# A two-layer trunk on one core: u tiles held two behind, low parts of weights made by POOL, output loads on SP

## The chip, the cores and the metric

The kernel runs on one core of one Trainium2 chip. Its engines are TensorE (PE, matrix products, with its weight loads PEld), VectorE (DVE), ScalarE (ACT), GpSimd (POOL) and SyncE (SP), which here only issues DMAs. Each engine works through its own list of instructions in order, and waits at an instruction until what it needs is there. The metric is the device time of one execution in microseconds (us), and of several executions the median.

## The reference

A trunk of two layers over a sequence of 1024 positions of width 1024. Layer 0 is a gated linear attention (GLA), layer 1 an S5 state space model; both have a cross attention into a memory beside the sequence mixer, a gate and an output projection.

```python
h = rms_norm(x, norm_w[i])                 # i = 0: GLA, i = 1: S5
u, z, xq = split_cols(h @ w_in, [2048, 3072, 1024])   # S5 layer
# S5: 128 groups of 16 columns with 64 complex states, in chunks of 128 steps
bu = einsum('bcgh,gph->bcgp', u, bb)       # into the states
x_t = ab * x_{t-1} + bu_t                  # recursion
y = Re(c x) + d * u
y = gelu(y); y = y * sigmoid(y @ w_glu + b_glu)
x = x + (concat([y, memory_attention(xq)]) * silu(z)) @ w_out[i]
```

After layer 1 a last RMSNorm gives the output. All is float32.

## The kernel before

A float32 product is made of three faster ones: both factors are split into a high part (rounded to a format that PE takes at full rate) and a low part (the rest), and high x high, high x low and low x high are summed (`mm3`, L78 to 86 in the class `Trunk`). For weights `unit()` does it: it loads a tile of 128x1024 (`wr`, three buffers, SP's queue, L78), ACT makes the high part `wh` (L69), and the low part `wl` is the subtraction `wr - wh` on DVE (L70). PE then does 48 products with such a unit, 24 for each half of the 1024 positions.

The order in which each engine does its instructions is made when the kernel is built: a scheduler simulates the program and puts instructions that are ready into an engine's list. Tiles come from pools with a number of buffers, and pools that are opened later reuse the memory of pools that are done; a tile then waits until the last use of what lay there. An explicit order (`behind`, `add_manual_dep`) keeps one instruction of an engine behind another. `self.made` is POOL's last store of the operators that it makes for the S5 stage (`od`, made by L770 to L775: two products into `op` and `opt`, their sum, a store).

The S5 stage, `s5()`, is where the diff lies:

- 16 units `w_su` make u, in two parts of eight tiles (`PARTS`; tiles 0 to 3 and 8 to 11, then the rest). Each tile is stored (`ud`, L919) and loaded again ordered by step (`uu`, L921).
- `states()` loads two operator tiles (`rt` into `rtp`, L902), lets PE multiply them with `uu` (L905, 16 products a tile, two blocks of eight), and ACT copies the result into the state tile `st`. The list `held` says how many tiles of u it lags behind the projections.
- The recursion over the 127 steps after the first runs on DVE, three operations a step (L932, L934, L936), for each part in two independent chains of 16 groups. The first chain of part 0 needs the tiles 0, 1, 8 and 9, the second the tiles 2, 3, 10 and 11.
- The outputs, per tile of u in two groups: loads of `uq` (u again), `tp` (into the tag `rtp`) and `ow` (from `od`), ACT and DVE make `xg` from the states, PE adds two products (L959 and L960), ACT makes the gelu (L961), SP stores (`y1`).
- 16 units `w_sz` make the gates: ACT a tanh (`zt`), DVE the product `zs` (L270), SP stores it.

Then `glu()` multiplies y with the last weight of the S5 layer. The scheduler mixes all of these: gates are projected while the recursion runs.

Of the kernel before, what the change touches and what calls it, by code (L numbers as in the profile page):

```python
# [8 lines left out]
F32 = mybir.dt.float32  # L9
# [7 lines left out]
P = 128  # L17
# [28 lines left out]
class Trunk:  # L46
# [19 lines left out]
    def split(self, h, l, src, scale=None, eng=None):  # L66
        nc = self.nc
        if scale is None:
            nc.scalar.copy(h, src)  # L69
            (eng or nc.vector).tensor_tensor(l, src, h.bitcast(F32), ALU.subtract)  # L70
        else:
            nc.scalar.activation(h, src, AF.Copy, scale=scale)
            nc.vector.scalar_tensor_tensor(l, src, scale, h.bitcast(F32), ALU.mult, ALU.subtract)

    def unit(self, src):

        raw = self.stream.tile([P, 1024], F32, tag="wr", name="wr")
        self.nc.sync.dma_start(raw, src)  # L78
        h = self.stream.tile([P, 1024], F32R, tag="wh", name="wh", bufs=2)
        l = self.stream.tile([P, 1024], F32R, tag="wl", name="wl", bufs=2)  # L80
        self.split(h, l, raw)
        return h, l

    def mm3(self, out, ah, al, bh, bl, first, last):
# [803 lines left out]
    def s5(self, xs, zs_d, y1_d):  # L888
# [3 lines left out]
        with ExitStack() as ctx:  # L892
            st = [self.pool(ctx, f"st{i}").tile([P, 2, 32, P + 1], F32, name=f"st{i}") for i in range(2)]
            sp = self.tags(ctx, "s5")
            for part in range(2):
# [13 lines left out]
                            nc.scalar.copy(st[part][hp, ri, g0:g0 + 4, 1:], pv[64 * ri:64 * ri + 64])  # L909

                held = []
                for j in self.PARTS[part]:
                    ub = sp.tile([P, 8, P], F32, tag="uy", name="uy", bufs=3)
                    u = self.unit(t["w_su"][j])
                    for hf in range(2):
                        ps = self.ps()
                        self.gemm(ps, u, xs[hf])
                        nc.scalar.copy(ub[:, :, 64 * hf:64 * hf + 64], ps.rearrange("p (s c) -> p s c", s=8))
                    nc.sync.dma_start(ud[j].rearrange("s p c -> p s c"), ub)  # L919
                    uu = sp.tile([P, 8, P], F32, tag="uu", name="uu", bufs=2)  # L920
                    nc.sync.dma_start(uu, by_step[j])  # L921
                    held.append((j, uu))
                    if len(held) > 1:
                        states(*held.pop(0))
                states(*held.pop())
                a2 = self.a2[:, :, :, 32 * part:32 * part + 32]
                chains = [slice(16 * i, 16 * i + 16) for i in range(2)]
                for c in range(2, P + 1):
# [8 lines left out]
            for part in range(2):  # L937
                for j in self.PARTS[part]:
                    half, jl = divmod(j, 8)
                    hp = slice(64 * half, 64 * half + 64)  # L940
                    yo = sp.tile([P, 8, P], F32, tag="uy", name="uy", bufs=3)
                    for q in range(2):
                        n, hb = 2 * jl + q, slice(4 * half, 4 * half + 4)
                        uq = sp.tile([P, 4, P], F32, tag="uq", name="uq", bufs=2)
                        loads = [nc.gpsimd.dma_start(uq, by_step[j][:, 4 * q:4 * q + 4, :])]  # L945
                        tp = sp.tile([P, 4, P], F32, tag="rtp", name="rtp", bufs=3)
                        loads.append(nc.gpsimd.dma_start(tp, self.tp_d[n][:, hb, :]))
                        ow = sp.tile([P, 4, P], F32, tag="ow", name="ow", bufs=2)
                        loads.append(nc.gpsimd.dma_start(ow, self.o_d[n][:, hb, :]))
                        for x in loads:  # L950
                            tc.add_manual_dep(x.ins, self.made.ins.name, mybir.DependencyInfo(mybir.DependencyClass.NoSync, mybir.DependencyReason.DATA), reason="order")
                        xg = sp.tile([P, 4, P], F32, tag="xg", name="xg", bufs=2)
                        g0 = 8 * (jl % 4) + 4 * q
                        nc.scalar.copy(xg[0:64], st[part][hp, 0, g0:g0 + 4, 0:P])  # L954
                        nc.vector.tensor_scalar(xg[64:P], st[part][hp, 1, g0:g0 + 4, 0:P], -1.0, None, ALU.mult)
                        ps = self.ps("a")
                        for g in range(4):
                            o = ps[:, g * P:(g + 1) * P]
                            nc.tensor.matmul(o, tp[:, g], uq[:, g], start=True, stop=False)  # L959
                            nc.tensor.matmul(o, ow[:, g], xg[:, g], start=False, stop=True)  # L960
                        nc.scalar.activation(yo[:, 4 * q:4 * q + 4, :], ps.rearrange("p (g c) -> p g c", g=4), AF.Gelu_apprx_tanh)  # L961
                    nc.sync.dma_start(y1_d[j].rearrange("s (h g) c -> (s h) g c", g=8), yo)
            for f in range(16):
                u = self.unit(t["w_sz"][f])
                for hf in range(2):
                    ps = self.ps()
                    self.gemm(ps, u, xs[hf])
                    z = sp.tile([P, HALF], F32, tag="zs5", name="zs5", bufs=2)
                    self.silu2(sp, z, ps, bufs=1)
                    nc.sync.dma_start(zs_d[f][:, hf * HALF:(hf + 1) * HALF], z)  # L970
# [229 lines left out]
```

## Time and profile before

| | before |
|---|---|
| median of three runs | 2624.02 us (2621.89 to 2625.38) |
| the profiled execution | 2626.52 us, its span 2624.6 us |
| mean granted clock of PE | 0.976 of full speed |
| PE busy | 2484.1 us, 95 % of the span |
| DVE busy | 1314.3 us, 50 % |
| ACT busy | 839.9 us, 32 % |
| POOL busy | 663.4 us, 25 % |

The span is from the first to the last instruction of the profiled execution; some 1.9 us lie around it. The busy times are means over a run with several stages: GLA up to about 1200 us, cross attention and projections to 1460, the S5 stage from 1460 to 2000, then the GLU and the output projection. An engine's share in one stage can be far from its mean.

### The profile page before, as it was taken

What the parts mean: (1) busy time and instruction counts of PE and PEld (TensorE: products, weight loads), DVE (VectorE), ACT (ScalarE), POOL (GpSimd) and SP (SyncE); (2) the same over time, 40 slices, a digit from 0 to 9 for tenths busy, and PEclk for the clock granted to TensorE, in tenths of its full rate; (3) what the DMA queues carried; (4) which work ended last, traced back from release to release, by engine and by line L of the source; (5) the groups of instructions that cost most, each with busy time, mean ns of one, the idle gap of its engine ahead of it and who ended that gap; (6) DMA issues with size and microseconds to landing.
All of it is one profiled execution on the core that took longest, in us unless ns stands there. A gap on an engine that the chain in (4) does not pass through costs nothing.

```text
span 2624.6 us, 32756 instructions
## 1 busy us (share of the span) xinstructions
PE 2484.1 (95%) x12000; PEld 2070.6 (79%) x12000; DVE 1314.3 (50%) x3306; ACT 839.9 (32%) x1426; POOL 663.4 (25%) x807
## 2 busy tenths in 40 slices
PE   7999999999999999998999689999948999999997
PEld 6888878888888887876788568888836888888887
DVE  7554353636364643566544207999844222232345
ACT  5422242525253423543222222322314111121144
POOL 6200000000000045725999990011210000000015
PEclk9999999999999999998999899999968999999999
DMA  6612112121213365665664665545847333355334
GB/s 224 196 39 72 63 65 72 57 81 65 81 65 101 125 244 194 194 204 154 201 182 146 162 182 177 165 155 171 280 141 221 120 121 122 121 179 199 130 127 162
DMA packets 201056, 377.69 MB, mean 144 GB/s; under 512 B 36832, under 2 KB 97888, under 8 KB 200896
## 3 DMA queue, kind: packets, MB, share of 16 engines
q1 hardware_dynamic: 160560, 303.09, 35.2%
q0 software_dynamic: 38032, 64.13, 8.4%
q10 hardware_dynamic: 2304, 8.39, 0.8%
q8 instruction: 94, 1.54, 0.2%
q14 instruction: 66, 0.54, 0.1%
HBM read 276.16 MB, written 95.55 MB: 142 GB/s over the span
## 4 chain that ended last, share of the span: by engine, by line
PE 80%; DMA 7%; DVE 5%; ACT 3%; POOL 3%; issue 1%; SPq 0%; POOLq 0%; DVEq 0%; ACTq 0%
PE ps_mm L86 69%; PE ps_b L86 3%; DMA ud<-uy 2%; PE ps_a L86 1%; PE ps_o L86 1%; DMA uu<-ud 1%; DVE wl L70 1%; PE ps_a L905 1%; PE ps_a L960 1%; DMA ow<-od 1%; PE ps_a L959 1%; POOL x L185 1%; PE ps_s L86 1%; DMA yr<-y 1%; DVE pd L932 1%
## 5 line engine op out<-in xcount | busy, mean ns | idle before, releaser
L86 PE MATMUL ps_mm<-X,wh 128*128 128x512 f32 (+1 forms) x4992 | 1531.3, 387 | 14.0 <-DVE zs L270 7.6
L86 PEld LDWEIGHTS ps_mm<-X,wh 128*128 128x128 f32 x4992 | 930.8, 189 | 201.9 <-DVE zs L270 8.2
L86 PE MATMUL ps_mm<-X,wl 128*128 128x512 f32 (+1 forms) x2496 | 965.4, 387 | 5.6 <-DVE wl L70 5.6
L70 DVE TENSOR_TENSOR wl<-wr,wh 128x1024 fp32r<-128x1024 f32 x260 | 350.6, 1349 | 462.5 <-ACT wh L69 461.6
L86 PEld LDWEIGHTS ps_mm<-X,wl 128*128 128x128 f32 x2496 | 471.8, 189 | 100.1 <-DVE wl L70 8.3
L69 ACT CAST wh<-wr 128x1024 fp32r<-128x1024 f32 x260 | 273.4, 1051 | 695.7 <-PE ps_mm L86 624.9
L127 POOL TENSOR_TENSOR nacc<-nacc,nsq 128x512 f32<-128x512 f32 (+1 forms) x30 | 40.0, 1333 | 577.8 <-ACT nsq L125 577.1
L511 POOL TENSOR_TENSOR rs<-ss,mhalf 128x1 f32<-128x1 f32 x32 | 20.3, 633 | 601.3 <-DVE ss L509 601.3
L932 DVE TENSOR_TENSOR pd<-a,st 128x64 f32<-128x64 f32 x508 | 126.3, 274 | 13.3 <-ACT st L909 7.0
L86 PE MATMUL ps_mm<-wh,X 128*128 128x512 f32 x384 | 125.0, 392 | 0.0
L270 DVE SCALAR_TENSOR_TENSOR zs<-zt,ps_mm 128x512 f32<-128x512 f32 x96 | 65.5, 682 | 104.9 <-ACT zt L269 104.8
L269 ACT ACTIVATE zt<-ps_mm 128x512 f32<-128x512 f32 x96 | 57.0, 594 | 189.0 <-PE ps_mm L86 169.3
L936 DVE TENSOR_TENSOR st<-st,pd 128x32 f32<-128x32 f32 x508 | 95.2, 214 | 6.1
L70 DVE TENSOR_TENSOR X<-yr,X 128x512 fp32r<-128x512 f32 x96 | 67.5, 728 | 48.8 <-ACT X L69 42.8
L960 PE MATMUL ps_a<-xg,ow 128*128 128x128 f32 x256 | 56.9, 310 | 36.6 <-ACT xg L954 24.5
L934 DVE TENSOR_TENSOR pd<-pd 128x32 f32<-128x32 f32 x508 | 86.9, 192 | 6.3
L1008 DVE SCALAR_TENSOR_TENSOR sg<-sg,y 128x512 f32<-128x512 f32 x32 | 22.0, 688 | 124.5 <-ACT sg L1005 124.5
L86 PEld LDWEIGHTS ps_mm<-wh,X 128*128 128x128 f32 x384 | 72.0, 188 | 15.0
L960 PEld LDWEIGHTS ps_a<-xg,ow 128*128 128x128 f32 x256 | 46.9, 224 | 39.0 <-ACT xg L954 26.7
L69 ACT CAST X<-yr 128x512 fp32r<-128x512 f32 x96 | 58.3, 620 | 57.4 <-DMA yr<-y 41.4
L945 POOL DMA_DIRECT2D uq<-ud x32 | 18.5, 577 | 224.6 <-PE ps_a L960 167.1
L86 PE MATMUL ps_mm<-wl,X 128*128 128x512 f32 x192 | 75.0, 391 | 0.0
(420 smaller groups left out, 3449.0 us busy)
## 6 DMA issues: line engine op xcount, KB each, us to landing
wr<-in_w_out SPq DMA_DIRECT2D x72, 512.0 KB, 4.0
yr<-y SPq DMA_DIRECT2D x96, 256.0 KB, 3.9
wr<-in_w_gv SPq DMA_DIRECT2D x32, 512.0 KB, 3.7
wr<-in_w_glu SPq DMA_DIRECT2D x32, 512.0 KB, 3.9
wr<-in_w_sz SPq DMA_DIRECT2D x26, 512.0 KB, 4.3
wr<-in_w_gz SPq DMA_DIRECT2D x24, 512.0 KB, 3.7
wr<-in_w_k SPq DMA_DIRECT2D x16, 512.0 KB, 4.4
wr<-in_w_v SPq DMA_DIRECT2D x16, 512.0 KB, 4.3
```

Of the source, the lines that this page charges most:

```text
L69: nc.scalar.copy(h, src)
L70: (eng or nc.vector).tensor_tensor(l, src, h.bitcast(F32), ALU.subtract)
L86: self.nc.tensor.matmul(out, a, b, start=start, stop=stop, skip_group_check=True)
L127: eng.tensor_tensor(acc[:, :width], acc[:, :width], sq[:, :width], ALU.add)
L185: nc.gpsimd.tensor_tensor(x, x, rbs, ALU.mult)
L269: self.nc.scalar.activation(th, ps, AF.Tanh, scale=0.5)
L270: self.nc.vector.scalar_tensor_tensor(out, th, 1.0, ps, ALU.add, ALU.mult)
L905: nc.tensor.matmul(pw[:, g * P:(g + 1) * P], rt[:, g], uu[:, 4 * q + g], start=True, stop=True)
L932: v.tensor_tensor(x, a2[:, :, :, g], prev, ALU.mult)
L934: v.tensor_tensor(x[:, :, 0, :], x[:, :, 0, :], x[:, :, 1, :], ALU.add)
L936: v.tensor_tensor(st[part][:, :, g, c], st[part][:, :, g, c], x[:, :, 0, :], ALU.add)
L960: nc.tensor.matmul(o, ow[:, g], xg[:, g], start=False, stop=True)
```

## The change

`split()` returns its subtraction, and `unit()` takes an engine for it. Where that is POOL, the subtraction stands in POOL's list behind `self.made`. POOL gets the third to eighth u tile of part 1 (six units) and all 16 gate units: 22 subtractions of 128x1024. `uu` has three buffers instead of two, and `states()` lags two tiles behind instead of one. The three loads of an output group, 96 in all, are issued by SP instead of POOL and no longer stand behind `self.made`.

```diff
--- before.py
+++ after.py
@@ -67,18 +67,20 @@
         nc = self.nc
         if scale is None:
             nc.scalar.copy(h, src)
-            (eng or nc.vector).tensor_tensor(l, src, h.bitcast(F32), ALU.subtract)
+            return (eng or nc.vector).tensor_tensor(l, src, h.bitcast(F32), ALU.subtract)
         else:
             nc.scalar.activation(h, src, AF.Copy, scale=scale)
             nc.vector.scalar_tensor_tensor(l, src, scale, h.bitcast(F32), ALU.mult, ALU.subtract)
 
-    def unit(self, src):
+    def unit(self, src, eng=None):
 
         raw = self.stream.tile([P, 1024], F32, tag="wr", name="wr")
         self.nc.sync.dma_start(raw, src)
         h = self.stream.tile([P, 1024], F32R, tag="wh", name="wh", bufs=2)
         l = self.stream.tile([P, 1024], F32R, tag="wl", name="wl", bufs=2)
-        self.split(h, l, raw)
+        ins = self.split(h, l, raw, eng=eng)
+        if eng is self.nc.gpsimd:
+            self.behind(ins, self.made)
         return h, l
 
     def mm3(self, out, ah, al, bh, bl, first, last):
@@ -909,20 +911,21 @@
                             nc.scalar.copy(st[part][hp, ri, g0:g0 + 4, 1:], pv[64 * ri:64 * ri + 64])
 
                 held = []
-                for j in self.PARTS[part]:
+                for i, j in enumerate(self.PARTS[part]):
                     ub = sp.tile([P, 8, P], F32, tag="uy", name="uy", bufs=3)
-                    u = self.unit(t["w_su"][j])
+                    u = self.unit(t["w_su"][j], nc.gpsimd if part and i > 1 else nc.vector)
                     for hf in range(2):
                         ps = self.ps()
                         self.gemm(ps, u, xs[hf])
                         nc.scalar.copy(ub[:, :, 64 * hf:64 * hf + 64], ps.rearrange("p (s c) -> p s c", s=8))
                     nc.sync.dma_start(ud[j].rearrange("s p c -> p s c"), ub)
-                    uu = sp.tile([P, 8, P], F32, tag="uu", name="uu", bufs=2)
+                    uu = sp.tile([P, 8, P], F32, tag="uu", name="uu", bufs=3)
                     nc.sync.dma_start(uu, by_step[j])
                     held.append((j, uu))
-                    if len(held) > 1:
+                    if len(held) > 2:
                         states(*held.pop(0))
-                states(*held.pop())
+                for x in held:
+                    states(*x)
                 a2 = self.a2[:, :, :, 32 * part:32 * part + 32]
                 chains = [slice(16 * i, 16 * i + 16) for i in range(2)]
                 for c in range(2, P + 1):
@@ -942,13 +945,11 @@
                     for q in range(2):
                         n, hb = 2 * jl + q, slice(4 * half, 4 * half + 4)
                         uq = sp.tile([P, 4, P], F32, tag="uq", name="uq", bufs=2)
-                        loads = [nc.gpsimd.dma_start(uq, by_step[j][:, 4 * q:4 * q + 4, :])]
+                        nc.sync.dma_start(uq, by_step[j][:, 4 * q:4 * q + 4, :])
                         tp = sp.tile([P, 4, P], F32, tag="rtp", name="rtp", bufs=3)
-                        loads.append(nc.gpsimd.dma_start(tp, self.tp_d[n][:, hb, :]))
+                        nc.sync.dma_start(tp, self.tp_d[n][:, hb, :])
                         ow = sp.tile([P, 4, P], F32, tag="ow", name="ow", bufs=2)
-                        loads.append(nc.gpsimd.dma_start(ow, self.o_d[n][:, hb, :]))
-                        for x in loads:
-                            tc.add_manual_dep(x.ins, self.made.ins.name, mybir.DependencyInfo(mybir.DependencyClass.NoSync, mybir.DependencyReason.DATA), reason="order")
+                        nc.sync.dma_start(ow, self.o_d[n][:, hb, :])
                         xg = sp.tile([P, 4, P], F32, tag="xg", name="xg", bufs=2)
                         g0 = 8 * (jl % 4) + 4 * q
                         nc.scalar.copy(xg[0:64], st[part][hp, 0, g0:g0 + 4, 0:P])
@@ -961,7 +962,7 @@
                         nc.scalar.activation(yo[:, 4 * q:4 * q + 4, :], ps.rearrange("p (g c) -> p g c", g=4), AF.Gelu_apprx_tanh)
                     nc.sync.dma_start(y1_d[j].rearrange("s (h g) c -> (s h) g c", g=8), yo)
             for f in range(16):
-                u = self.unit(t["w_sz"][f])
+                u = self.unit(t["w_sz"][f], nc.gpsimd)
                 for hf in range(2):
                     ps = self.ps()
                     self.gemm(ps, u, xs[hf])
```

How the lists of the engines change, at the four places that matter for what follows. SP, where the state operators are loaded (`rtp<-rt`); in brackets the semaphores that an instruction waits for, DMASW those of POOL's queue, DMAHW those of SP's. Before:

```order
L902 DMA rtp_13228<-rt0_3415 128x512 [waits DMAHW0_49,DMASW0_49]
L343 DMA y1_23_125<-y_12965 128x512 [waits DVE_49]
L902 DMA rtp_13237<-rt1_3416 128x512 [waits DMAHW2_49,DMASW6_49,PE_49]
L902 DMA rtp_13308<-rt2_3417 128x512 [waits DMAHW3_49,DMASW4_49,Activation_49]
L343 DMA y1_22_124<-y_13053 128x512 [waits DMAHW4_49,DVE_49]
L343 DMA y1_23_125<-y_13063 128x512 [waits DMAHW5_49,DVE_49]
L919 DMA ud0_13070<-uy_13098 128x8x128 [waits DMAHW6_49,Activation_49]
L921 DMA uu_13161<-ud0_13070 128x1024 [waits DMAHW6_49,DMAHW4_49,DMAHW7_49,PE_49,Pool_49]
```

And with the change:

```order
L921 DMA ud4_13074<-uy_14767 128x8x128 [waits DMAHW5_49,Activation_49]
L921 DMA ud5_13075<-uy_14829 128x8x128 [waits Activation_49]
L904 DMA rtp_13290<-rt0_3415 128x512 [waits DMAHW7_49,DMASW0_49]
L904 DMA rtp_13299<-rt1_3416 128x512 [waits DMASW4_49,DMASW5_49,DMASW3_49,DMASW6_49,DMASW2_49,DMASW7_49,DMASW1_49,DMAHW0_49,DMASW0_49,Pool_49]
L904 DMA rtp_13370<-rt2_3417 128x512 [waits DMAHW1_49]
L78 DMA wr_15132<-in_w_su 128x1024 [waits DMAHW2_49,Pool_49]
L948 DMA uq_16427<-ud0_13070 128x512 [waits DMASW5_49,DMASW4_49,DMASW6_49,DMASW3_49,DMASW7_49,DMASW2_49,DMAHW3_49,DMASW1_49,DMASW0_49]
L952 DMA ow_16434<-od0_3447 128x512 [waits DMASW6_49,DMAHW4_49,DMASW5_49,DMASW0_49]
L948 DMA uq_16452<-ud0_13070 128x512 [waits DMAHW5_49]
L78 DMA wr_15212<-in_w_su 128x1024 [waits DMAHW6_49,Pool_49]
L952 DMA ow_16456<-od1_3448 128x512 [waits DMAHW7_49,DMASW4_49]
L904 DMA rtp_13379<-rt3_3418 128x512 [waits DMAHW0_49,PE_49]
```

Before, the loads follow the last stores of the cross attention (`y1`), and none of the rows that load `rtp` waits for POOL. With the change, the second of them, `rtp_13299`, waits for POOL and for all of the DMAs of POOL's queue; the loads of u for the outputs (`uq`, `ow`) follow close behind.

PE, at the second block of states (L905, L907 with the change; products of a unit with `wh` and `wl` around it). Before:

```order
L86 MATMUL ps_mm<-X,wh 128x512 x2
L86 MATMUL ps_mm<-X,wl 128x512
L86 MATMUL ps_mm<-X,wh 128x512 x2
L905 MATMUL ps_a<-uu,rtp 128x128 x8
L86 MATMUL ps_mm<-X,wl 128x512
L86 MATMUL ps_mm<-X,wh 128x512 x2
L86 MATMUL ps_mm<-X,wl 128x512
```

With the change, the first and the second block:

```order
L88 MATMUL ps_mm<-X,wh 128x512
L907 MATMUL ps_a<-uu,rtp 128x128 x8
L88 MATMUL ps_mm<-X,wh 128x512
L88 MATMUL ps_mm<-X,wl 128x512 x2
L88 MATMUL ps_mm<-X,wh 128x512 x2
L88 MATMUL ps_mm<-X,wl 128x512
L88 MATMUL ps_mm<-X,wh 128x512 x2
L88 MATMUL ps_mm<-X,wl 128x512
L88 MATMUL ps_mm<-X,wh 128x512 x2
L88 MATMUL ps_mm<-X,wl 128x512
L88 MATMUL ps_mm<-X,wh 128x512 x2
L88 MATMUL ps_mm<-X,wl 128x512
```

Before, one block of states stood in each unit of 48 products, from the third u tile on (some 30 rows apart). Now the first stands in the eleventh unit, behind 48 products each of the third to tenth, and the next follow 20 products apart, so that two stand in a unit.

DVE, in the recursion (`pd0`, `st0` are the chains of part 0, `pd1` or `st1` those of part 1). Before, soon after its beginning:

```order
L936 TENSOR_TENSOR st0_13089<-st0_13089,pd0_13830 128x2x16
L932 TENSOR_TENSOR pd0_13838<-a2_3410,st0_13089 128x64
L934 TENSOR_TENSOR pd0_13838<-pd0_13838 128x2x16
L70 TENSOR_TENSOR wl_14833<-wr_14830,wh_14832 128x1024
L936 TENSOR_TENSOR st0_13089<-st0_13089,pd0_13838 128x2x16
L932 TENSOR_TENSOR pd0_13846<-a2_3410,st0_13089 128x64
```

With the change, in part 1:

```order
L935 TENSOR_TENSOR pd1_16232<-a2_3410,st1_13093 128x64
L935 TENSOR_TENSOR pd0_16351<-a2_3410,st1_13093 128x64
L937 TENSOR_TENSOR pd1_16232<-pd1_16232 128x2x16
L937 TENSOR_TENSOR pd0_16351<-pd0_16351 128x2x16
L939 TENSOR_TENSOR st1_13093<-st1_13093,pd1_16232 128x2x16
L939 TENSOR_TENSOR st1_13093<-st1_13093,pd0_16351 128x2x16
L935 TENSOR_TENSOR pd1_16240<-a2_3410,st1_13093 128x64
```

Before, 88 steps of one chain stand alone (three operations a step) with a subtract of `wl` every 40 rows or so, then 39 steps of two chains in turn (six operations), 88 and 39 so again across the parts, and 88 alone. With the change 15 stand alone, 112 in turn, 15 in turn across the parts, 112 in turn, 15 alone, and no `wl` stands among them until the GLU's first.

POOL, behind the making of the operators. Before:

```order
L774 TENSOR_TENSOR op<-op,opt 128x512
L775 DMA od_3462<-op 2x64x512
L945 DMA uq<-ud_13070 128x512
L949 DMA ow<-od_3447 128x512
L945 DMA uq<-ud_13070 128x512
L949 DMA ow<-od_3448 128x512
```

With the change:

```order
L776 TENSOR_TENSOR op<-op,opt 128x512
L777 DMA od_3462<-op 2x64x512
L70 TENSOR_TENSOR wl<-wr,wh 128x1024 x22
L129 TENSOR_TENSOR nacc<-nacc,nsq 128x512 x6
```

The loads are gone from the list, and 22 subtractions stand in their place.

## Rows read from the trace of the kernel before

**Rows 1.** Windows: us; busy us (count) of PE, PEld, DVE, ACT, POOL; clock, DMA, GB/s

```profile
1450.00:1500.00 50.00, 30.20 (x136) 24.08 (x134) 10.47 (x16) 9.75 (x18) 48.95 (x48) 0.86 0.66 174
...
1550.00:1600.00 50.00, 42.31 (x189) 35.35 (x188) 22.68 (x78) 13.32 (x21) 28.62 (x27) 0.90 0.64 190
...
1700.00:1750.00 50.00, 50.00 (x264) 42.83 (x263) 49.75 (x291) 16.01 (x24) 7.63 (x14) 1.00 0.53 169
...
1900.00:1950.00 50.00, 20.82 (x108) 18.55 (x106) 30.41 (x123) 8.10 (x14) 7.86 (x15) 0.69 0.35 118
```

**Rows 2.** Chain of waits, S5 stage and (last row) whole run: start us, us, what

```profile
1462.06 2.54 PE ps_mm L86 x10
...
1477.89 13.90 DMA ud<-uy
...
1602.44 1.78 PE ps_a L905 x16
...
1734.96 70.09 PE ps_mm L86 x309
...
1938.82 5.62 DMA ow<-od
...
1969.88 5.40 DMA ow<-od
...
1998.57 566.70 PE ps_mm L86 x2510
```

**Rows 3.** Recursion's third line: duration ns min/median/max, first and last start

```profile
L936 DVE TENSOR_TENSOR st<-st,pd x508: 202/215/223, 1576.2 to 1931.9; 128x32 f32<-128x32 f32 x170
```

**Rows 4.** DVE's timeline in the recursion: start us, us, operation, count

```profile
1574.97 1.22 DVE L934 TENSOR_TENSOR pd<-pd 128x32 f32<-128x32 f32 x1
...
1576.48 0.28 DVE L932 TENSOR_TENSOR pd<-a,st 128x64 f32<-128x64 f32 x1
...
1576.79 0.19 DVE L934 TENSOR_TENSOR pd<-pd 128x32 f32<-128x32 f32 x1
...
1577.27 0.28 DVE L932 TENSOR_TENSOR pd<-a,st 128x64 f32<-128x64 f32 x1
...
1753.57 0.46 DVE L932 TENSOR_TENSOR pd<-a,st 128x64 f32<-128x64 f32 x2
...
1754.42 0.46 DVE L932 TENSOR_TENSOR pd<-a,st 128x64 f32<-128x64 f32 x2
```

**Rows 5.** Subtract of wl on DVE, 1250 to 1574 us, then 1620 to 1900

```profile
L70 DVE TENSOR_TENSOR wl<-wr,wh x21: 1216/1508/4593, 1254.6 to 1565.9; 128x1024 fp32r<-128x1024 f32 x21
...
L70 DVE TENSOR_TENSOR wl<-wr,wh x21: 1212/1218/1226, 1628.2 to 1896.8; 128x1024 fp32r<-128x1024 f32 x21
```

**Rows 6.** Gate product of the S5 stage on DVE, whole run, by line

```profile
L270 DVE SCALAR_TENSOR_TENSOR zs<-zt,ps_mm x96: 671/681/689, 147.0 to 1910.0; 128x512 f32<-128x512 f32 x96
```

**Rows 7.** POOL's timeline at the recursion's start

```profile
1574.87 1.28 POOL L774 TENSOR_TENSOR op<-op,opt 128x512 f32<-128x512 f32 x1
```

**Rows 8.** DMA issues, median us to landing: whole run, then 1440 to 1580 us

```profile
rtp<-rt SPq DMA_DIRECT2D x32, 256.0 KB, 5.0
...
ow<-od POOLq DMA_DIRECT2D x32, 256.0 KB, 6.0
...
rtp<-rt SPq DMA_DIRECT2D x15, 256.0 KB, 8.8
```

**Rows 9.** POOL's two-input operations: ns min/median/max; last by line: busy us, mean ns

```profile
L774 POOL TENSOR_TENSOR op<-op,opt x32: 1262/1284/2165, 1425.3 to 1574.9; 128x512 f32<-128x512 f32 x32
...
L801 POOL TENSOR_TENSOR op<-op,opt x32: 735/741/1617, 1219.5 to 1415.8; 128x256 f32<-128x256 f32 x32
...
L70 POOL TENSOR_TENSOR X<-nxn,X 128x512 fp32r<-128x512 f32 x16 | 30.3, 1902 | 14.8 <-ACT X L69 14.8
```

**Rows 10.** Time of one issue of a load, ns min/median/max, SP and POOL

```profile
L902 SPq DMA_DIRECT2D rtp<-rt x32: 319/386/2856, 1450.9 to 1692.1; - x32
...
L949 POOL DMA_DIRECT2D ow<-od x32: 538/538/773, 1585.7 to 1979.3; - x32
```


## The prediction

> **What bounds the kernel now.** I read the page first: TensorE (PE) is busy 95 % of the span, VectorE (DVE) 50 %. So the kernel is bound by PE nearly everywhere, and a change can gain only where PE stands still. The table of 50 us windows shows two such places, both in the S5 stage that the diff touches [rows 1]. From 1450 to 1600 us (three windows, of which the first and the last are shown) PE is busy 30 to 42 us of 50, and from 1900 to 1950 us only 21. In between it is full, and so is DVE, at 49.75 of 50 from 1700 to 1750: two engines at the limit together.
>
> Next the chain of waits, to see what PE stands for [rows 2]. In the first place each tile of u goes out to DRAM (`ud`) and comes back ordered by step (`uu`), up to 13.9 us a leg, and PE's state products (L905) wait for it. In the second the chain is DVE's last recursion step (at 1931.9 [rows 3]), then twelve output groups one behind the other, which wait for loads of `ow` and `uq`; the GLU's first product starts at 1998.57, and PE works without a gap worth naming from there on. So the end of the S5 stage, and with it the whole run (566.7 us of PE work follow), is set by when the recursion ends plus 66.7 us. The recursion ran from about 1574.6 (its second operation starts at 1574.97 [rows 4]) to 1931.9, 357 us. What moves that end moves the time one to one.
>
> **How the 357 us are made.** DVE's timeline [rows 4] gives a step of one chain alone: 1576.48 to 1577.27, 0.79 us; and of two chains interleaved: 1753.57 to 1754.42, 0.85 us for both. A step alone is latency, so a partner is nearly free. The order of before has 88 steps of the first chain alone, 39 pairs, 88 pairs, 39 pairs, 88 alone: 176 x 0.79 + 166 x 0.85 = 280. Added: 21 subtracts of `wl` by DVE at about 1.13 net of the gap they fill (1.22 each [rows 5]) = 24; some 30 gate products `zs` at 0.60 net of 0.68 [rows 6] = 18. That is 322; the other 35 us are the small work for the outputs (`xg`) and waits.
>
> **The change, part by part.**
>
> *Three `uu` tiles, states two tiles behind.* They would give the round trip more cover, but the order shows something else. One more `uu` buffer shifts the addresses of what is opened after it, and the second load of the state operators (`rtp_13299`) now waits for POOL; by the count of the semaphore that is POOL's last operator product `opt`, which ended as the sum behind it began, at 1574.87 [rows 7]. Every states block needs such loads, so none runs before about 1580. PE does the u tiles of the third to tenth unit without a states block between: 24 + 8 x 48 products at 0.2268 us (70.09 us for 309 [rows 2]) from 1462.06 [rows 2] end about 1555, then PE stands some 25 us. From 1450 to 1600 PE lost some 36 us of 150 anyway (19.8 and 7.7 in the two windows of [rows 1]), so this idle takes the place of another; it isn't added.
>
> Then the order has two states blocks per unit, 20 products between: 20 x 0.2268 + 1.78 [rows 2] = 6.3 us a tile. Its two loads of 256 KB took 5.0 us median [rows 8], just hidden. The first block stands behind 26 products of the first unit whose low part POOL makes (below); I put its end at 1588. The sixth tile, the last that the first chain needs, is at 1588 + 5 x 6.3, and with ACT's copies about **1622**: the recursion starts **47 us later** (before 1574.6). The second chain follows two tiles on, 1634, not some 90 us on as before.
>
> *That is what pays it back.* The order of DVE now has 15 steps alone, 112 pairs, 15 pairs across the two parts, 112 pairs, 15 alone: 30 single, 239 pairs, so 30 x 0.79 + 239 x 0.85 = 227 us against 280, **53 less**.
>
> *Low parts by POOL.* 22 subtracts of 128x1024 leave DVE. POOL's price isn't in the trace. Its 128x512 two-input product has a median of 1.28, the 128x256 one 0.74 [rows 9]; the line through both gives 1.28 + 512 x 0.0021 = 2.4 us. The far bound is twice POOL's own 128x512 subtract beside a busy DVE, 2 x 1.90 = 3.8 [rows 9]. I take 2.4, since POOL's products run in the same stage and on the same kind of operands, the other subtract in another stage. Does DVE run on meanwhile? One row says no [rows 4, 7]: the second recursion operation takes 0.19, but 1.22 when it meets POOL's `op` (1574.87, 1.28 us), and ends with it, at 1576.2. And the subtract on DVE takes a median of 1.51 (up to 4.59) while POOL makes operators, 1.22 when POOL is mostly silent [rows 5]. So I charge each POOL subtract in the recursion wholly to DVE. Four fall before the recursion starts, 18 within: 18 x 2.4 = **43 us**, where DVE's own would cost 18 x 1.13 = 20. The lower bound is nothing (DVE runs on), the upper 18 x 3.8 = 68.
>
> The Trainium skill, "SBUF — State Buffer", section "SBUF: two separate sides", says that a GpSimd operation and a DVE operation with two SBUF inputs share a port pair that the one which starts first holds for its whole instruction; the trace agrees (1.22 against 0.19). By that rule the 43 us stand and the edit slows the engine that it relieves; were the one row chance, they would be 0, which is rival B.
>
> *Outputs loaded on SP.* 96 loads leave POOL's queue. They no longer wait for POOL's operator making by order, but in SP's queue they stand among stores of `zs` (wait for DVE) and weight loads (now wait for POOL). In the recursion this lies under it. After it PE still has 12 output groups in turn; the loads of `ow` in the chain start 10.35 us apart per two groups (1938.82 to 1969.88, three steps [rows 2]). An issue costs 0.54 on POOL, 0.39 on SP, and landing was 5.0 on SP's queue for such a tile, 6.0 for `ow` on POOL's [rows 8, 10]: about 1.2 a pair, five pairs, **6 us less**. Bounds: 0 (the stores of y between them eat it) to 10.
>
> The Trainium skill, "DMA: Bandwidth & Descriptors", section "Issuing engines are not separate DMA queues", says that the engine which starts a DMA changes only the time to initiate it. By that the landing would stay, and only the issue would shrink, 3 x 0.15 a group, so that the sum would be some 3 us less favourable; the rows differ in landing too, so I keep 6.
>
> *The sum.* Recursion: 227 + 43 (POOL) + one DVE split 1.2 + 18 (`zs`) + 13 of `xg` and waits = 302, from 1622: ends 1924, 8 earlier. I leave 13 of the 35 of before because its single-chain stretches waited for states, which now lie ahead of the pairs. With the tail's 6 it makes **-14**. The profiled run took 2626.5 and lies 2.5 above the median of 2624.0; the difference goes onto the median: **2610 us**. Own range of this case: start of the recursion 5 either way, `xg` and waits 9 to 20, tail 0 to 10: 2596 to 2622.
>
> **Rivals.**
>
> *B. POOL's subtract doesn't hold DVE.* For it: only one recursion step in the trace meets a POOL product. Against: that row, and the 1.51 and 4.59. DVE's chain would be 43 shorter, and then PE is the bound again: from 1580, 22 units of 10.9 and 24 state and output blocks of about 2 us give 1869, with the output groups' waits some 1880 to 1888, 45 to 50 earlier: **2575**.
>
> *C. Loads of state operators are the pace.* In 1440 to 1580 such loads took 8.8 us [rows 8]; if POOL's last stores and the loads of `uq` and `ow`, which SP now has ahead of them, keep it so, a tile takes about 8.5 instead of 6.3, and the recursion starts 5 x 2.2 = 11 to 13 later: **2622**, no change that can be told. A measurement of this kernel tells about 0.2 %, 5 us, from none.
>
> *D, the slower side. POOL's subtract is long.* The same full block, but at the 3.8 us of POOL's own subtract [rows 9]: 18 x 1.4 = 25 more, so +11: **2635**. It decides from about 3.2 us on, where 18 x 0.8 eats the 14. For it: POOL must take the port between DVE's operations that follow each other without a gap. Against: POOL would wait at most for one recursion operation, 0.28.
>
> *E. The later start is not there*: if the second operator load waits for an earlier operation of POOL than I read, the states run as early as before and the result is that of B at its best, 2575; the order speaks against it.
>
> **How the numbers follow.** Chances: A 0.55, B and E together 0.13, C 0.14, D 0.18. The prediction is A's time. The range runs from 2577, which leaves out half of B, to 2635, which leaves out half of D. Faster by over 0.2 % (under 2618.8): most of A, 0.50, and B: 0.63. Within 0.2 %: A's upper end 0.04 and most of C, 0.12: 0.16. Slower: D and a rest of A and C: 0.21.
>
> **What would show it.** Right: PE empty from about 1555 to 1580; the first L932 operation near 1622; pairs at 0.85 nearly throughout; 18 recursion operations of over 2 us beside a POOL subtract; end of the recursion about 1924; the GLU's first product about 1984. B shows short recursion operations beside POOL and PE full to the end; C a start after 1630; D POOL subtracts over 3.2 us. I would be wholly wrong if PE's order is stalled by something that the order alone doesn't show, such as a weight load in SP's queue behind a load that waits for POOL, since with three weight buffers each wait there reaches PE two units later.

## The result, and the profile after

The changed kernel takes 2602.61 us, median of four runs (2598.61 to 2606.35), against 2624.7 before (2621.89 to 2625.84). The ratio is 0.9917, 95 % interval 0.9898 to 0.9936: 22 us less, where 14 were forecast. The profiled execution took 2604.83, its span is 2603.0.

The windows of the changed kernel answer to [rows 1] (us; busy us and count of PE, PEld, DVE, ACT, POOL; clock, DMA share, GB/s):

```profile
1500.00:1550.00 50.00, 50.00 (x222) 41.42 (x221) 7.00 (x4) 10.02 (x14) 49.02 (x46) 1.00 0.73 200
1550.00:1600.00 50.00, 28.20 (x133) 23.15 (x132) 0.00 (x0) 8.89 (x14) 33.72 (x29) 0.76 0.57 164
...
1700.00:1750.00 50.00, 48.67 (x213) 39.58 (x211) 50.00 (x266) 8.07 (x11) 9.73 (x4) 1.00 0.23 78
...
1900.00:1950.00 50.00, 39.22 (x239) 35.19 (x239) 24.02 (x89) 17.92 (x31) 0.00 (x0) 0.90 0.85 279
```

PE no longer limps through the u tiles: it is full to 1550, then stands some 22 us, nearly all in one piece. At 1700 DVE is at 50.00 and PE at 48.67: DVE is full in the middle of the stage and PE is not.

The recursion's first and third line (duration ns min/median/max, first and last start), which answer to [rows 3]:

```profile
L935 DVE TENSOR_TENSOR pd<-a,st x508: 259/272/2486, 1621.9 to 1918.1; 128x64 f32<-128x64 f32 x170
...
L939 DVE TENSOR_TENSOR st<-st,pd x508: 202/213/2422, 1622.5 to 1919.1; 128x32 f32<-128x32 f32 x170
```

It starts at 1621.9, 47 later than before, and ends 297 us on, at 1919.3. The largest duration of each line is new: 2.4 to 2.5 us where the median is 0.2 to 0.3. The timelines of POOL and DVE show what it is (start us, us, operation):

```profile
1577.58 4.67 POOL L70 TENSOR_TENSOR wl<-wr,wh 128x1024 fp32r<-128x1024 f32 x2
...
1625.41 2.43 POOL L70 TENSOR_TENSOR wl<-wr,wh 128x1024 fp32r<-128x1024 f32 x1 [12.10 <-ACT wh L69]
1641.88 2.48 POOL L70 TENSOR_TENSOR wl<-wr,wh 128x1024 fp32r<-128x1024 f32 x1 [14.04 <-ACT wh L69]
...
1887.82 2.38 POOL L70 TENSOR_TENSOR wl<-wr,wh 128x1024 fp32r<-128x1024 f32 x1 [10.48 <-ACT wh L69]
```

```profile
1625.63 2.29 DVE L939 TENSOR_TENSOR st<-st,pd 128x32 f32<-128x32 f32 x1
...
1641.59 0.33 DVE L939 TENSOR_TENSOR st<-st,pd 128x32 f32<-128x32 f32 x2
1641.83 2.65 DVE L935 TENSOR_TENSOR pd<-a,st 128x64 f32<-128x64 f32 x2
```

Whichever recursion operation meets POOL's subtract lasts until that ends: 1625.63 + 2.29 = 1627.92 beside 1625.41 + 2.43 = 1627.84. Of the 22 subtracts four lie ahead of the recursion and 18 within, the first at 1625.41 and the last at 1887.82.

The chain of waits, to compare with [rows 2] (start us, us, what):

```profile
1579.98 6.90 PE ps_mm L88 x20
1586.88 1.78 PE ps_a L907 x16
1588.67 4.55 PE ps_mm L88 x20
1593.22 1.78 PE ps_a L907 x16
...
1941.64 5.04 DMA ow<-od
...
1948.84 5.72 DMA ow<-od
...
1974.78 25.35 PE ps_mm L88 x99
```

PE starts again at 1579.98, when POOL's first low part is there; the row of PE's waits from 1550 to 1600 (us in total, times, longest) says for what it stood:

```profile
PE ps_mm L88 <- POOL wl L70: 21.3, 1, 21.3
```

The states then come every 6.34 us. The GLU starts at 1974.78, 23.8 earlier than before, 55.5 after the end of the recursion instead of 66.7. From there on the run is 628 us long, 2 more than before.

### The profile page after: what moved, and what is told of

It reads as the page before. It is cut to its first block, busy times and chain, and to the rows that moved or that the text cites. A ratio compares the mean times of both kernels' runs of the same rounds, so it can differ in the third digit from the quotient of the medians.

```text
span 2603.0 us, 32721 instructions
## 1 busy us (share of the span) xinstructions
PE 2483.0 (95%) x12000; PEld 2066.7 (79%) x12000; DVE 1285.9 (49%) x3284; ACT 840.6 (32%) x1426; POOL 663.0 (25%) x733
## 5 line engine op out<-in xcount | busy, mean ns | idle before, releaser
L88 PE MATMUL ps_mm<-X,wl 128*128 128x512 f32 (+1 forms) x2496 | 966.0, 387 | 28.0 <-POOL wl L70 21.3
L70 DVE TENSOR_TENSOR wl<-wr,wh 128x1024 fp32r<-128x1024 f32 x238 | 326.5, 1372 | 429.0 <-ACT wh L69 426.7
L70 POOL TENSOR_TENSOR wl<-wr,wh 128x1024 fp32r<-128x1024 f32 x22 | 53.2, 2420 | 259.5 <-ACT wh L69 236.1
L937 DVE TENSOR_TENSOR pd<-pd 128x32 f32<-128x32 f32 x508 | 95.2, 219 | 1.2
L960 PE MATMUL ps_a<-uq,rtp 128*128 128x128 f32 x256 | 55.0, 299 | 19.4 <-DMA uq<-ud 13.7
L1006 ACT ACTIVATE sg<-ps_mm,bgh 128x512 f32<-128x512 f32 x32 | 21.9, 685 | 147.0 <-PE ps_mm L88 147.0
```

What stands on the lines that cost most here:

```text
L70: return (eng or nc.vector).tensor_tensor(l, src, h.bitcast(F32), ALU.subtract)
L88: self.nc.tensor.matmul(out, a, b, start=start, stop=stop, skip_group_check=True)
L937: v.tensor_tensor(x[:, :, 0, :], x[:, :, 0, :], x[:, :, 1, :], ALU.add)
```

## The experiments

All times are medians of each kernel's runs, all ratios are against the kernel before, run on the same chip in turn (its median there 2619 to 2622). In the table the start and the end of the recursion, and the tail from there to the GLU (its last activation `x251h`), are of the profiled execution; where PE, not the tail, ends the stage, the tail has no meaning and is left out.

| kernel | us | ratio (95 %) | recursion | length | tail |
|---|---|---|---|---|---|
| before | 2624.7 | 1 | 1574.6 to 1932.1 | 357 | 66 |
| changed | 2602.6 | 0.9917 (0.9898 to 0.9936) | 1621.9 to 1919.3 | 297 | 55 |
| only_sp | 2604.8 | 0.9942 (0.9925 to 0.9959) | 1568.2 to 1920.5 | 352 | 51 |
| only_two_behind | 2644.0 | 1.0091 (1.0061 to 1.012) | 1658.2 to 1937.3 | 279 | 79 |
| only_pool | 2633.2 | 1.0052 (1.0034 to 1.007) | 1565.5 to 1927.2 | 362 | |
| all_dve | 2617.3 | 0.9991 (0.9978 to 1.0004) | 1659.6 to 1938.3 | 279 | 52 |
| gates_dve | 2589.5 | 0.9889 (0.9868 to 0.9909) | 1625.7 to 1912.3 | 287 | 52 |
| gates_twice | 2644.1 | 1.0091 (1.007 to 1.0112) | 1623.9 to 1955.4 | 332 | 59 |
| one_pool | 2590.2 | 0.9877 (0.9859 to 0.9896) | 1629.4 to 1915.3 | 286 | 54 |
| loads_pool | 2625.5 | 1.0013 (0.9999 to 1.0027) | 1626.9 to 1926.3 | 299 | 69 |
| st1_late | 2566.7 | 0.9795 (0.9774 to 0.9816) | 1573.5 to 1861.6 | 288 | |
| gates_dve_st1_late | 2563.1 | 0.9781 (0.9762 to 0.98) | 1573.5 to 1854.1 | 281 | |
| one_pool_st1_late | 2568.5 | 0.9803 (0.9781 to 0.9824) | 1594.9 to 1864.7 | 270 | |
| all_dve_st1_late | 2617.1 | 0.9986 (0.9969 to 1.0003) | 1652.8 to 1921.8 | 269 | |

My theory was that of the prediction: the later states let the chains run as pairs, POOL's subtracts hold DVE, the tail shrinks a little. The rivals: the loads are the whole gain; POOL relieves DVE.

### One part of the change alone

Loads on SP alone, to the kernel before:

```diff
-                        loads = [nc.gpsimd.dma_start(uq, by_step[j][:, 4 * q:4 * q + 4, :])]
+                        nc.sync.dma_start(uq, by_step[j][:, 4 * q:4 * q + 4, :])
...
-                            tc.add_manual_dep(x.ins, self.made.ins.name, mybir.DependencyInfo(mybir.DependencyClass.NoSync, mybir.DependencyReason.DATA), reason="order")
```

> The kernel before with one part of the change, the output loads on SP. The lists of PE, DVE and ACT are those of before. My theory (the gain has two sources, the pairing of the chains that the later states bring, and the shorter tail): the recursion stays as it was, 1574.6 to 1931.9, and only the tail from its end to the GLU's first product shrinks from 66.7 to the 55.5 us that it has with the change: 11 less, about 2613 us. Rival (the loads are the whole gain): 22 less, 2602.

Measured: 0.9942, some 15 us less; the tail 51. That lies between the 11 of my theory and the 22 of the rival. It is most of what the whole change brings, and its interval overlaps that of the change, so the rival isn't excluded by this run. The chain of this kernel in its tail:

```profile
1923.14 3.32 DMA ow<-od
...
1928.62 4.78 DMA ow<-od
...
1933.54 0.46 PE ps_a L958 x2
1933.99 0.22 PE ps_a L957 x2
...
1935.35 0.11 SPq L945
...
1935.56 5.32 DMA ow<-od
...
1943.04 4.61 DMA ow<-od
```

And one step of the chain before, to compare:

```profile
1938.82 5.62 DMA ow<-od
...
1944.58 0.77 PE ps_a L960 x2
1945.35 0.43 PE ps_a L959 x2
...
1947.78 0.42 POOL uq L945
...
1948.50 0.19 POOL rtp L947
...
1949.03 6.79 DMA ow<-od
```

The loads that PE waits for start 5.5, 6.9 and 7.5 us apart per two groups, 6.6 in the mean, where they were 10.35 apart on POOL's queue [rows 2]. Three things make the 3.7 us, as means of three steps of each chain. From PE's last product in the chain to the start of the load it is 1.56 us before and 0.21 here: 1.35. The products of a step (12 in the chain before, 14 here) take 2.92 us and 1.82: 1.1. A pair of them takes 0.43 before and 0.22 here, which are the two levels of PE's clock (1.2 and 2.4 GHz). The landings in the chain take 5.74 and 4.47: 1.3. The mean granted clock from the end of the recursion to the GLU was 0.76 before, with PE busy for 42.4 of 66.5 us, and 0.90 here, with 35.1 of 51.4.

Two behind alone:

```diff
-                    uu = sp.tile([P, 8, P], F32, tag="uu", name="uu", bufs=2)
+                    uu = sp.tile([P, 8, P], F32, tag="uu", name="uu", bufs=3)
...
-                    if len(held) > 1:
+                    if len(held) > 2:
```

> The kernel before with one part of the change, three uu tiles and states two tiles behind. Its second load of state operators waits for POOL as in the changed kernel, and the order puts the first states block behind all 16 u units (PE row 7388 against 7085). My theory: the recursion starts near 1632 + 5 x 6.3 + 4 = 1667, has nearly all steps in pairs (about 26 x 0.79 + 241 x 0.85 = 225, 14 subtracts on DVE 16, gates 18, rest 13: 272 us), ends near 1939, tail 66.7 as before: 8 later than before, about 2632. Rival (holding the states back is the gain by itself): about 2610 or less.

Measured: 1.0091, 24 us slower. The recursion is 279 us long, 7 over the forecast, and starts at 1658, 9 ahead of it, so that its end, 1937, is met (1939) by two misses that cancel. The 79 us of the tail, 13 over the 66 of before, did not come out. Holding the states back is a loss by itself, but the pairs pay for all but 5 us of a start 84 us later: most of the loss lies in the tail.

POOL alone:

```diff
-                    u = self.unit(t["w_su"][j])
+                    u = self.unit(t["w_su"][j], nc.gpsimd if part and i > 1 else nc.vector)
...
-                u = self.unit(t["w_sz"][f])
+                u = self.unit(t["w_sz"][f], nc.gpsimd)
```

> The kernel before with one part of the change, the 22 subtracts on POOL. The order has 200 single steps and 154 pairs, and the states early as before. My theory (each POOL subtract holds DVE for its 2.42 us): the recursion starts at 1575, takes 200 x 0.79 + 154 x 0.85 = 289, 22 x 2.42 = 53, gates 18, rest 35, so some 395 against 357: 30 to 40 slower, about 2660. Rival (POOL relieves DVE): 21 x 1.13 = 24 less, about 2600.

Measured: 1.0052, 14 us slower: against the rival, and of the sign of the theory, but by less than half of the forecast and not by its path. The recursion became 362 us long, not 395, and ended at 1927.2, 5 us earlier than before, so a later end of it is not what made the run slower. I had kept all of the 35 us of waits of before and added the subtracts; most likely these lie in part where DVE had waited, which was not tried apart. What I didn't forecast is a piece that PE lost: 26.5 us in one wait for ACT's copy `uy`, since in ACT's list an `xg` stood ahead that waited 41.3 us for the recursion. After it PE is the bound: it is at 50.00 of 50 from 1950 to 2000, and the GLU starts at 2005.8.

### One part of the change undone

All low parts on DVE again:

```diff
-                    u = self.unit(t["w_su"][j], nc.gpsimd if part and i > 1 else nc.vector)
+                    u = self.unit(t["w_su"][j])
...
-                u = self.unit(t["w_sz"][f], nc.gpsimd)
+                u = self.unit(t["w_sz"][f])
```

> The changed kernel with all low parts on DVE again. The order puts the states behind all 16 u units (PE row 7388), as with two behind alone. My theory: recursion from about 1667 to 1939, then the short tail of 55.5: GLU's first product near 1995, 20 later than with the change, about 2621. So POOL's subtracts would help, though they hold DVE, only because the first of them stops PE and thereby pulls the states forward in the order. Rival (they only cost, 18 x (2.42 - 1.13) = 23): 2580. Rival (they relieve DVE): about 2625, with the recursion's start as it is with the change, 1622.

Measured: 0.9991, no change from before, the recursion from 1659.6 to 1938.3. It is the first answer, to 4 us (2617 beside 2621). Without POOL's subtracts PE's list runs through all 16 u units before the first states, and the chain shows it as one piece of 167 us (start us, us, what):

```profile
1457.25 167.33 PE ps_mm L88 x737
```

So POOL's subtracts help, though each holds DVE. The next run asks for how many that is true.

```diff
-                    u = self.unit(t["w_su"][j], nc.gpsimd if part and i > 1 else nc.vector)
+                    u = self.unit(t["w_su"][j], nc.gpsimd if part and i == 2 else nc.vector)
...
-                u = self.unit(t["w_sz"][f], nc.gpsimd)
+                u = self.unit(t["w_sz"][f])
```

> The changed kernel with a single low part on POOL, that of the third u tile of part 1 (behind POOL's last operator store); the other 21 on DVE. Order: states from PE row 7091 (7085 with the change), 30 single steps and 239 pairs, 20 subtracts on DVE in the recursion. My theory: one such subtract is enough to pull the states forward, since PE's list stops there in the order; recursion 227 + 20 x 1.13 + 18 + 13 = 281 from 1624, ends near 1905: 2585 to 2592, as with the six u units on POOL. Rival (POOL must take work from DVE): near 2617, as with all on DVE.

Measured: 0.9877, better than the change with its 22. One subtract, behind POOL's last store, puts the recursion's start at 1629, close to the 1622 of the change. Its interval and that of the change miss each other by 0.0002. The 16 of the gates alone:

```diff
-                u = self.unit(t["w_sz"][f], nc.gpsimd)
+                u = self.unit(t["w_sz"][f])
```

> The changed kernel with the low parts of the 16 gate units on DVE again, those of the six u units still on POOL. PE's list of states blocks and the pairs of the recursion (32 single, 238 pairs) are those of the changed kernel. My theory (a POOL subtract holds DVE for 2.42 us, DVE's own costs 1.13 net): 16 x (2.42 - 1.13) = 21 less, recursion from 1622 to about 1899, about 2582 us, unless PE becomes the bound first. Rival (POOL relieves DVE): 16 x 1.13 = 18 more, about 2621.

Measured: 0.9889, 0.0028 under the change (7 us, with intervals that overlap), the recursion 11 us shorter than with the change, not 21. The sign is that of the theory; the net price of a POOL subtract against one of DVE is 11 / 16 = 0.7 us here, not 1.3. And each of them twice (the second writes the same values again):

```diff
+            if n > 1:
+                eng.tensor_tensor(l, raw, h.bitcast(F32), ALU.subtract)
```

> The changed kernel with the POOL subtract of each gate unit done twice (the second writes the same values again). Lists of PE and DVE as with the change. My theory (hold): 16 x 2.42 = 39 more in the recursion, about 2641. Rival (DVE runs on beside POOL): within a few us of 2603. A result near half of that would say that part of the second subtracts falls beside DVE operations that read only one operand from where POOL does, or besides PE waits.

Measured: 1.0091; the recursion is 34 us longer than with the change, 2.1 us for each of 16. With the long operations of the profile this says that DVE doesn't run on beside POOL. Rival B falls.

The loads on POOL again:

```diff
-                        nc.sync.dma_start(uq, by_step[j][:, 4 * q:4 * q + 4, :])
+                        loads = [nc.gpsimd.dma_start(uq, by_step[j][:, 4 * q:4 * q + 4, :])]
...
+                            tc.add_manual_dep(x.ins, self.made.ins.name, mybir.DependencyInfo(mybir.DependencyClass.NoSync, mybir.DependencyReason.DATA), reason="order")
```

> The changed kernel with one part undone, the output loads on POOL again. Lists of PE and DVE as with the change. My theory: the tail grows from 55.5 to the 66.7 of before or a little more, since POOL issues the load of ow 1.24 us after that of uq where SP needs 0.41: 11 to 15 more, 2614 to 2618. Rival (the place of the loads counts only while the recursion runs): within 4 us of 2603. Rival (POOL's subtracts wait behind its loads): over 2625.

Measured: 1.0013, the whole gain gone. 0.0096 of ratio are 25 us, more than the 11 to 15 that I expected; in the profiles 14 are the tail, 69 against 55, and 7 the recursion's later end. POOL's and SP's lists in the tail show the difference. POOL, with its loads (start us, us, operation):

```profile
1956.58 0.54 POOL L948 DMA_DIRECT2D uq<-ud  x1 [3.22 <-PE ps_a L962]
1957.11 0.54 POOL L950 DMA_DIRECT2D rtp<-tp  x1
1957.64 0.54 POOL L952 DMA_DIRECT2D ow<-od  x1
```

SP, in the changed kernel:

```profile
1941.23 0.32 SPq L948 DMA_DIRECT2D uq<-ud  x1
1941.64 0.38 SPq L952 DMA_DIRECT2D ow<-od  x1
1942.12 0.38 SPq L963 DMA_DIRECT2D y<-uy  x1
1942.55 0.42 SPq L950 DMA_DIRECT2D rtp<-tp  x1
```

The load that PE waits for, `ow`, goes out 0.41 us after `uq` on SP, where it is second, and 1.06 on POOL, where it is third and each issue lasts 0.54. The granted clock in the tail is 0.85 here and 0.93 in the changed kernel.

A third pair of kernels differs in the loads alone: only_two_behind has them on POOL, all_dve on SP, with all low parts on DVE in both. There SP gains 0.0100, 26 us; the recursion ends at the same time (1937.3 and 1938.3), and the tail goes from 79 to 52, with a granted clock of 0.74 and 0.96. So in three pairs the loads give 15, 26 and 25 us.

### The wait of the states for POOL taken away

In these the state tile of part 1 gets its memory after `uy`, `uu` and `rtp`, so that their addresses no longer lie on POOL's last operator tiles.

```diff
-            st = [self.pool(ctx, f"st{i}").tile([P, 2, 32, P + 1], F32, name=f"st{i}") for i in range(2)]
-            sp = self.tags(ctx, "s5")
+            s_ = lambda i: self.pool(ctx, f"st{i}").tile([P, 2, 32, P + 1], F32, name=f"st{i}")
+            st = [s_(0)]
+            sp = self.tags(ctx, "s5", order=("uy", "uu", "rtp"))
+            st.append(s_(1))
```

> The changed kernel with only the opening of the tiles moved (state tile of part 1 behind uy, uu and rtp), all 22 subtracts still on POOL. It undoes the late start alone. My theory: recursion from 1574, 254 x 0.85 = 216, some 20 x 2.42 = 48, gates 18, rest 13: 295, ends near 1869, then the short tail, of which PE's gates take some: 2565 to 2580. So the wait of the state operators for POOL would cost the changed kernel some 30 us. Rival (PE stood there anyway, nothing is lost): 2603.

Measured: 0.9795. With nothing else changed in the program (the lists follow from it) the recursion starts at 1573.5 instead of 1621.9, all steps are pairs, and the run is 32 us shorter than the changed kernel (0.0122 of ratio). The later start was the price of the change. The recursion ends 58 us earlier, so the time no longer follows its end one to one.

With the gates' low parts on DVE besides:

> The changed kernel with the gates' low parts on DVE, and the state tile of part 1 opened behind uy, uu and rtp, so that these have their memory without waiting for POOL's last products. Order: the states start at the fourth u unit (PE row 6723), eight blocks by row 7061, and all 254 steps are pairs. My theory: recursion from about 1585, 254 x 0.85 = 216, 15 subtracts 17, gates 18, two POOL subtracts 5, rest 13: 269, to about 1855; by then PE has not done the gates (PE alone would need to about 1880), so PE is the bound, and the GLU starts near 1925 to 1940: about 2555 to 2570. Rival (the wait for POOL cost nothing, since PE stood there anyway): as with the gates on DVE alone, about 2582.

Measured: 0.9781, the fastest kernel of this study, 58 us under before. Its windows at the end of the stage:

```profile
1800.00:1850.00 50.00, 50.00 (x222) 41.40 (x222) 50.00 (x290) 10.11 (x14) 0.00 (x0) 1.00 0.28 93
1850.00:1900.00 50.00, 49.60 (x314) 44.35 (x312) 16.39 (x44) 20.03 (x34) 0.00 (x0) 1.00 0.85 280
```

The recursion ends at 1854, DVE drops to 16 of 50, and PE still has work, at 49.60: there PE is the bound again. A wait for POOL is left there, that of the recursion's first operation, which waits 21.48 us for POOL's last `opt`:

```profile
1573.47 0.27 DVE L937 TENSOR_TENSOR pd<-a,st 128x64 f32<-128x64 f32 x1 [21.48 <-POOL opt L775]
```

With one low part on POOL:

> The same single low part on POOL, with the state tile of part 1 opened behind uy, uu and rtp. Order: states from PE row 6723, 253 pairs. My theory: PE is the bound as with the six u units on POOL (2563), so within 3 us of that, 2560 to 2566; two POOL blocks fewer in the recursion (2 x 1.3) can't show. Rival (recursion still the bound): 3 to 5 less, 2558.

Measured: 0.9803, not told apart from the two before it: between 1, 6 and 22 subtracts on POOL the ratio differs by 0.0022, within the intervals. The recursion is the shortest of them, 270 us, but starts 21 later in this profile. And with none:

> As the kernel before it, but all low parts on DVE, none on POOL. Order: eight states blocks by PE row 7061 as there, the next only from 7171 and 7403 on; 253 of the steps are pairs. My theory: the recursion of part 0 starts near 1585 or a little before, as nothing waits for POOL's end; part 1 later: near 2560 to 2575. Rival (POOL must take a share of the low parts for DVE to keep up): over 2590.

Measured: 0.9986. Here my expectation failed. The states of part 0 were there early, but DVE did not begin. PE's last block of them, and DVE's timeline:

```profile
1577.24 4.14 PE L909 MATMUL ps_a<-uu,rtp 128*128 128x128 f32 x16 [4.13 <-DMA uu<-ud]
```

```profile
1640.76 1.22 DVE L70 TENSOR_TENSOR wl<-wr,wh 128x1024 fp32r<-128x1024 f32 x1 [9.65 <-ACT wh L69]
1651.64 1.23 DVE L70 TENSOR_TENSOR wl<-wr,wh 128x1024 fp32r<-128x1024 f32 x1 [9.66 <-ACT wh L69]
1652.78 0.46 DVE L937 TENSOR_TENSOR pd<-a,st 128x64 f32<-128x64 f32 x2
```

Seven subtracts stand ahead of the recursion in DVE's list, the last at 1651.64; each waits for its unit, and the recursion waits behind them, 71 us after its states were done. I had read PE's list and not that of DVE.

## Why the prediction was right

- **The idle of PE and the start of the recursion** came as forecast: PE stands some 22 us (25 forecast) to 1579.98 (1580), the states come every 6.34 us (6.3), the recursion starts at 1621.9 (1622). The cause of the idle was another than the prediction gave: PE stood 21.3 us for POOL's first low part, not for the operator loads. Both wait for the end of POOL's operators, so that the time came out in part by luck. That the idle "isn't added" was half the truth. Against before PE lost no more there; but st1_late shows that without the wait for POOL 32 us more were to be had.
- **Pairs**: 53 us less was the largest gain of the sum. The recursion took 297 us (302 forecast).
- **Low parts by POOL**: the line through two rows gave 2.4; 22 subtracts have a median of 2.41, and each of the 18 within the recursion holds DVE (gates_twice: 2.1 us for each more). That this part helps at all, through the order, I hadn't said: of the 22 one is enough, and the other 21 cost 0.004 of ratio, 10 us (one_pool). Rivals B and D fall, the first by the 18 long operations, the second by the 2.41; C falls with the 6.34.
- **The tail** was the term that was mis-sized: 6 less forecast, "about 1.2 a pair, five pairs", 11 measured in the profile. With the loads undone it is 14, and the time 25. A pair gained 3.7 us in the three steps of only_sp: 1.35 on the way from the last product to the load, where the 1.2 has room for one issue's 0.15; 1.3 in the landings, where it has 1.0; and 1.1 in PE's products, which ran at the higher level of the clock and for which it has no term. In all three pairs of kernels the granted clock in the tail is higher with the loads on SP (0.90, 0.96 and 0.93 beside 0.76, 0.74 and 0.85). Whether it gives time of its own or only follows from the shorter waits, no run here pulls apart.
- **The rule on the port pair** (the Trainium skill, "SBUF — State Buffer", section "SBUF: two separate sides") held: each of the 18 subtracts within the recursion has one recursion operation of over 2 us beside it.
- **The rule on the issuing engine** (the Trainium skill, "DMA: Bandwidth & Descriptors", section "Issuing engines are not separate DMA queues"), that it changes only the time to initiate a DMA, would have made the forecast gain smaller, and the gain was larger. That doesn't contradict it: over all loads of `ow` from 1900 on, the median landing is 5.1 us before and 5.4 in loads_pool, 4.9 in only_sp and 5.1 in the changed kernel, so no run here shows that the engine sets the landing. The 1.0 that the sum took for it came from medians over the whole run.
- **The sum**: the end of the recursion came 13 earlier (8 forecast), the tail 11 (6), the GLU at 1974.8 (1984).
- **The attribution needs a correction.** The sum put 8 of 14 on the recursion, and nothing on the loads while it runs. The single parts say: loads alone 15 us, the other two without the loads nothing (1.0013), all together 22. In the profile of only_sp the recursion also ends 12 earlier, with the same lists of DVE, half of it by an earlier start; in loads_pool it ends 7 later than with the change; between only_two_behind and all_dve it doesn't move. These are single profiles, and how much of such a difference is the loads' stays open. So the step that failed is the 8 us of the recursion as a gain of its own: the pairs and the delayed start cancel more nearly than I had them, and that its end came out at all is in part luck. What is left for them of the 22, with the loads on SP, is 7 us by the medians of the ratios (0.9942 and 0.9917), with intervals that overlap.
- **"What moves that end moves the time one to one"** holds only while the tail, and not PE, ends the stage. In only_pool the recursion ended 5 us earlier and the run was 14 slower; in st1_late it ended 58 before that of the change and the run gained 32.

## What to carry to other kernels

One more buffer can move the addresses of everything opened behind it onto tiles of another engine that is not done; read the waits in the new order, and let tiles that are needed late take those addresses. Giving an engine's work to a second one that holds the first while it runs is no relief; here it helped by its place in the order alone, and one instruction did that as well as 22. An earlier end of one chain is worth its time only until another engine is the bound. When a chain of short loads sets the end, what counts is how soon the load that is waited for goes out: its place among its neighbours on the queue, and the time of an issue. Where PE waited longer, its granted clock was lower as well, and the products between the loads took 0.43 us a pair instead of 0.22.

## What the runs showed that was not expected

- A POOL subtract of 128x1024 takes 2.41 us, DVE's 1.22, and a DVE operation with two inputs from SBUF that meets it ends with it (18 times within the recursion).
- Replacing the 16 gate subtracts on POOL by DVE's own saved only 0.7 us each in the recursion, where 2.4 - 1.1 was expected; doubling them cost 2.1 each. The two don't add up to one price. Where in the list of DVE the subtract falls seems to matter; it was not tried.
- The operator loads that wait for POOL held up SP (three of them took it 17.7 us, from 1558.4 on), but not PE: what PE stood for was a low part.
- The mean granted clock rose from 0.976 before to 0.988 in the fastest kernel. In the changed kernel it was 0.76 in the window with PE's 22 us of idle and 1.00 in the window before it, where PE was full.
